# A written-out schedule with other costs, one more attention tile turned by VectorE, and another buffer for the first left operand

## The chip, the cores and the metric

The kernel runs on one core of a Trainium2 chip. The metric is device time in microseconds of one execution; of several executions the median is given. A profile is one more execution, taken by the hardware profiler; its span runs from the first to the last instruction. The five engines named below are TensorE (PE; its weight loads are shown as PEld), VectorE (DVE), ScalarE (ACT), GpSimd (POOL) and SyncE (SP), which issues all of this kernel's DMAs.

## The reference, cut to what matters

One layer of a hybrid encoder over a prompt of 1024 tokens and a sample of 32, width 1024. Normalised rows are multiplied by `w_in` into eight blocks of 512 columns (q, k, v and gate g of the head groups A and B, 8 heads of 64 each). Group A is chunked band attention with a relative bias, group B is stick-breaking attention. Both outputs are gated, multiplied by `w_out`, normalised and added; a last gated term with `w_ple_gate` and `w_ple` follows. Everything is float32.

```python
def stick_breaking(q, k, v, q_pos, k_pos):          # group B
    z = jnp.einsum('bqhd,bkhd->bhqk', q, k).astype(jnp.float32) * ATTN_SCALE
    causal = (k_pos[None, :] < q_pos[:, None])[None, None]
    log_1m = jnp.where(causal, jax.nn.log_sigmoid(-z), 0.0)
    after = lax.cumsum(log_1m, axis=3, reverse=True) - log_1m
    w = jnp.where(causal, jnp.exp(jax.nn.log_sigmoid(z) + after), 0.0).astype(v.dtype)
    return jnp.einsum('bhqk,bkhd->bqhd', w, v)
```

## The kernel before, in words

**Precision.** Every operand x of a matmul is split into hi (x rounded to the type fp32r) and lo (x - hi). ScalarE mostly casts hi, VectorE or GpSimd subtracts for lo, and TensorE adds up three products, or two where the halves are stacked.

**Stages.** First the rows are normalised and turned (`ptx`), and a part of the `w_ple` products is made (`ple`). Then come eight pairs of heads in the order A0, B0, A1, B1, A2, B2, A3, B3. While a pair's attention runs, the projections of the next pair (`mm_k..`, `mm_q..`, `mm_v..`, three column groups of 24 matmuls each) are woven in; beside the last pair stand the gates `mm_gA` and `mm_gB`. Last come the remaining `ple` products, the output projection (`o..P`) and the gate (`g..P`), each as seven products of half-size blocks (Strassen's way) for pairs of row tiles.

**Attention of one head** (`attention`, L790). A query tile i has 128 rows. `scores(i)` (L826) multiplies it with its keys into PSUM (tag S); for B, ScalarE takes a sigmoid into a tile `om`, VectorE scans it from right to left (cumulative product), and GpSimd subtracts neighbours into a tile `be`, the weights. `weights_t(i)` (L876) turns the weights, since the values product needs keys on partitions: TensorE transposes each 128x128 block into PSUM (tag T, named `ptw`), ScalarE casts hi (`wTh`), VectorE subtracts lo (`wTl`). For the tiles listed in `ROUND` (L31) another way is taken: VectorE transposes 32x32 squares from `be` back into `om`, one DMA writes `om` to DRAM (`swap`), four DMAs read it back into `be` with the squares in their turned places, and ScalarE and VectorE split it from there. `values(g)` (L926) multiplies four tiles at once with v (`PV`, `ot`). Tiles of `om` and `be` lie in two rings of fixed size (`Arena`, L208); a new tile waits for the last use of those that it overlaps. A B head's tile i has (i + 1) x 128 columns. The last head takes its tiles from 7 down to 0.

**The order of the work.** Nothing is issued as it is written. A `Recorder` (L264) collects all operations with their dependences; `cost` (L338) gives each a busy time and a time `late` from the end of that to the result; `order` (L372) then lists them: the engine that is free earliest takes the ready operation with the lowest key, where a result for another engine counts `SEM` = 60 ns more and for TensorE `MARGIN` = 400 ns more. On TensorE, attention goes before projections. The list is emitted as it stands, so each engine's instructions, and SP's DMAs, run in that fixed order. Line L450 in the profile is the one that emits everything; so instructions are known by their tiles' names.

**The output projection's start.** Raw weights `wo` are loaded into two buffers of tag `ao` in the pool `fb`, which opens when the attention's pool closes, and are split from there (L1451 on; `woB` and `woT` in turn, four each, two halves in each). The left operands of the even row tile (`A11o`, `A12o`, `S2o`, ...) are taken by `Side.room` (L1539) in turn from the same two buffers of `fb`, or from one buffer of `fa`, a pool that opens when the normalised rows are needed no more, behind the last gate projection.

Of the kernel before, what the change touches and what calls it, by code (L numbers as in the profile page):

```python
# [8 lines left out]
F32 = mybir.dt.float32  # L9
# [18 lines left out]

ROUND = {"A": ((4,),(6,)), "B": ((4,),(6,))}  # L31
LAG_T = 2
LAG_V = 2
SPACE_S = 0.1
# [229 lines left out]
class Recorder:  # L264
# [72 lines left out]
    @staticmethod  # L337
    def cost(eng, method, args, kw, writes, reads):  # L338

        out = writes[0] if writes else None  # L340
        n = out.free() if isinstance(out, View) else 1
        psum = any(isinstance(v, (View, Segments)) and v.buf.psum for v in reads)
        if eng == "PE":
            if method == "transpose":
                return (109 if args[1].shape[0] > 64 else 62), 165
            return max(109.0, 2.5 + 0.449 * args[2].free()) * (1 if args[2].buf.dtype == F32R else 4), 165
        if eng == "ACT":
            return (165 if psum else 200) + 0.83 * n + (190 if "accum_out" in kw else 0), 0
        if eng == "DVE":
            if method == "tensor_tensor_scan":  # L350
                return 155 + 2.08 * n, 0
            if method == "tensor_copy" and not psum:
                return 155 + 0.53 * n, 0
            if method == "scalar_tensor_tensor":
                return 210 + 1.04 * n, 0
            return 155 + 1.04 * n + (83 if method == "tensor_tensor_reduce" else 0), 0
        if eng == "POOL":
            if method == "tensor_tensor":
                if n == 1:
                    return 400, 0  # L360
                return 190 + (1.77 if out.buf.dtype == F32 else 2.15) * n, 0
            if method == "tensor_scalar":
                return 255 + 0.86 * n, 0
            return 100 + 0.82 * n, 0
        size, run = 4, 0
        for v in (out, args[1]):
            if isinstance(v, View) and v.buf.pool is not None:
                size, run = 4 * v.shape[0] * v.free(), 4 * v.shape[-1]
        return ISSUE, max(size / DMA_RATE, size / run * (8.5 + 0.0365 * run) / 16)


    def order(self):  # L372

        import heapq
        for place, old in self.turns:
            place.after.update(x[0] for x in old.uses)
        users = {id(o): [] for o in self.ops}
        for o in self.ops:
            o.left, o.ready = len(o.after), 0.0
            for a in o.after:  # L380
                users[id(a)].append(o)
        names = ("PE", "ACT", "DVE", "POOL", "SP", "CTL")
        free = dict.fromkeys(names, 0.0)
        soon = {e: [] for e in names}
        now = {e: [] for e in names}
        for o in self.ops:
            if not o.left:
                heapq.heappush(soon[o.eng], (0.0, o.key, id(o), o))
        out, port, line = [], 0.0, 0.0
        while len(out) < len(self.ops):  # L390
            best = None
            for e in names:
                if now[e]:
                    t = free[e]
                elif soon[e]:
                    t = max(free[e], soon[e][0][0])
                else:
                    continue
                if best is None or t < best[0]:
                    best = (t, e)  # L400
            t, e = best
            while soon[e] and soon[e][0][0] <= t:
                _, key, n, o = heapq.heappop(soon[e])
                heapq.heappush(now[e], (key, n, o))
            o = heapq.heappop(now[e])[2]
            if o.shared and e == "DVE" and port > t + DVE_SET:
                held = [x for x in now[e] if not x[2].shared]
                if held:
                    heapq.heappush(now[e], (o.key, id(o), o))
                    pick = min(held)  # L410
                    now[e].remove(pick)
                    heapq.heapify(now[e])
                    o = pick[2]
            o.at = t
            if e == "CTL":
                done = t
            elif e == "SP":
                free[e] = t + o.busy
                line = max(line, t + o.busy + DMA_NS) + o.late
                done = line + DMA_MARGIN  # L420
            else:
                if o.shared:
                    t = max(t, port - (DVE_SET if e == "DVE" else POOL_SET))
                    port = t + o.busy
                free[e] = t + o.busy
                done = t + o.busy + o.late
            out.append(o)
            for u in users[id(o)]:
                if u.eng == e and e != "SP":
                    r = t if e == "CTL" else free[e]  # L430
                else:
                    r = done + (0 if u.eng == "CTL" else SEM + (MARGIN if u.eng == "PE" else 0))
                u.ready = max(u.ready, r)
                u.left -= 1
                if not u.left:
                    heapq.heappush(soon[u.eng], (u.ready, u.key, id(u), u))
        return out
# [18 lines left out]
def stream_step(  # L456
# [19 lines left out]
    def scratch(shape, name):  # L476
# [29 lines left out]
        out=maskb, in_=maskb, pattern=[[-1, P]], base=0, channel_multiplier=1,  # L506
# [29 lines left out]
    def load_w(j):  # L536

        if j >= len(order) or j in raws:
            return
        kind, p = order[j]  # L540
        c0 = NAMES.index(kind) * 512 + p * P
        raws[j] = []
        for kh in range(2):
            raw = wpool.tile([P, 4, P], F32, tag="wr", name=f"wr_{kind}{p}_{kh}", bufs=4)
            dma(raw, w_in[0, kh * 512:(kh + 1) * 512, c0:c0 + P].rearrange("(k p) c -> p k c", p=P))
            raws[j].append(raw)

    def ensure(j):

        if j >= len(order) or j in loaded:  # L550
            return
        load_w(j)
        kind, p = order[j]
        loaded[j] = []
        if j == 2:
            pair = [ringl.tile([P, 2, 4, P], f"w{x}_{kind}{p}") for x in "hl"]
        for kh in range(2):
            raw = raws[j][kh]
            if j == 2:
                hi, lo = (x[:, kh] for x in pair)  # L560
            else:
                hi = wpool.tile([P, 4, P], F32R, tag="wh", name=f"wh_{kind}{p}_{kh}", bufs=4)
                lo = wpool.tile([P, 4, P], F32R, tag="wl", name=f"wl_{kind}{p}_{kh}", bufs=4)
            (nc.gpsimd.tensor_copy if j < 3 else nc.scalar.copy)(hi, raw)
            nc.gpsimd.tensor_tensor(lo, raw, f(hi), ALU.subtract)
            loaded[j].append((hi, lo))
# [223 lines left out]
    def attention(ab, p, h):  # L790
# [16 lines left out]

        together = {i: g for g in ROUND[ab] for i in g}
        whole, done_with = {}, []
# [4 lines left out]
        def rooms(i):  # L814

            more = ab == "B"
            g = together.get(i, (i,))
            if g not in whole:
                n = sum(cost(x) for x in g) * P
                whole[g] = ring0.tile([P, n + more * len(g)], f"om{nm}_{i}"), ring1.tile([P, n], f"be{nm}_{i}")  # L820
            k, n = g.index(i), cost(i) * P
            a = sum(cost(x) for x in g[:k]) * P
            w0, w1 = whole[g]
            return w0[:, a + more * k:a + more * k + n + more], w1[:, a:a + n]
# [379 lines left out]
    for n in range(-1, 8):  # L1204
        a = len(order)
        if n < 7:
            ab, p = pairs[n + 1]
            order += [(k + ab, p) for k in "kqv"]
        for _ in range(share.get(n, 0)):
            order.append(gates.pop(0))  # L1210
        span.append((a, len(order)))

    done = set()
# [309 lines left out]
    class Side:  # L1523
# [14 lines left out]

        def room(self, n, key):  # L1539
            if self.pair == 0:  # L1540
                one = Side.taken % 3 == 2
                Side.taken += 1
                x = (fa if one else fb).tile([P, 2, KT, P], F32R, tag="ao", name=f"{key}{self.nm}", bufs=1 if one else 2)
                return x[:, 0], x[:, 1]
            return [wpool.tile([P, KT, P], F32R, tag=tag, name=f"{tag}{key}{self.nm}", bufs=4) for tag in ("wh", "wl")]
# [321 lines left out]
```

## Time and profile before

| | |
|---|---|
| median of 3 executions | 806.38 us (805.48 to 808.88) |
| the profiled execution | 808.3 us, span 806.5 us |
| mean granted TensorE clock in it | 0.996 |
| busy: TensorE, VectorE, ScalarE, GpSimd | 784.5, 575.5, 507.8, 436.8 us |
| moved by DMA | 161.08 MB in 160971 packets, mean 200 GB/s |

The profiled execution takes 1.8 us more than its span. A busy time is the share of the span in which at least one instruction of that engine runs; matmuls overlap, so a group's busy time is less than its count times the mean duration. In the rows of groups, "xcount | busy, mean ns | idle before" follow the tiles and shapes; the idle time is that of the engine just ahead of these instructions, with what ended it. In rows of time, the start in us is followed by the length of the merged instructions. A row of waits has the total, the number of times and the longest.

### The profile page before, as it was taken

The page shows a single profiled execution, that of the slowest core. Times are in us where ns is not written, and L with a number is a line of the kernel's source. Part 1 is how long each engine was busy: PE and PEld are TensorE (multiplying, and loading weights), DVE is VectorE, ACT ScalarE, POOL GpSimd, SP SyncE. Part 2 cuts the span into 40 slices and gives each one's busy share as a digit, 9 for nine tenths or more (in the row PEclk, how much of TensorE's full clock was granted, in tenths as well). Part 3 has the DMA queues.
Part 4 walks back from the last instruction along what each step waited for, and adds up shares of the span by engine and source line. Part 5 has one row for each costly group of instructions (what it writes and reads, how often), then busy time and mean ns, then how long its engine had stood idle before and what let it go on. Part 6 is the DMA issues. An engine that isn't in the chain of part 4 may idle for free.

```text
span 806.5 us, 14268 instructions
## 1 busy us (share of the span) xinstructions
PE 784.5 (97%) x4646; PEld 722.4 (90%) x4646; DVE 575.5 (71%) x1007; ACT 507.8 (63%) x1063; POOL 436.8 (54%) x503
## 2 busy tenths in 40 slices
PE   8999999999999999999999999999998999999997
PEld 6899989999889998999999989999996877888786
DVE  6627678886588897778896878766355687586565
ACT  5636675676476655785666685543337867876741
POOL 5613656873556676234660336777541537699523
PEclk9999999999999999999999999999999999999999
DMA  8419987668877749745545667774579767659743
GB/s 275 152 38 276 232 247 243 168 181 237 229 210 228 203 147 272 190 137 152 125 115 159 153 171 231 218 211 151 156 236 329 245 188 231 216 179 343 249 137 131
DMA packets 160971, 161.08 MB, mean 200 GB/s; under 512 B 39153, under 2 KB 120793, under 8 KB 160898
## 3 DMA queue, kind: packets, MB, share of 16 engines
q1 hardware_dynamic: 160898, 160.18, 67.0%
q8 instruction: 37, 0.61, 0.3%
q14 instruction: 36, 0.29, 0.1%
HBM read 99.23 MB, written 52.49 MB: 188 GB/s over the span
## 4 chain that ended last, share of the span: by engine, by line
PE 84%; ACT 5%; POOL 3%; DVE 3%; DMA 2%; issue 2%; SPq 1%; DVEq 0%; ACTq 0%; POOLq 0%
PE mm_gB L450 6%; PE mm_gA L450 6%; PE mm_qA L450 5%; PE mm_kA L450 5%; PE mm_vA L450 5%; PE mm_qB L450 4%; PE mm_kB L450 4%; PE SB L450 4%; PE PVB L450 4%; PE mm_vB L450 3%; PE PVA L450 3%; PE SA L450 3%; PE ptwB L450 3%; PE o0P L450 3%; PE o1P L450 2%; PE g0P L450 2%
## 5 line engine op out<-in xcount | busy, mean ns | idle before, releaser
L450 DVE TENSOR_TENSOR_SCAN om<-om,SB 128x384 f32<-128x384 f32 (+5 forms) x96 | 95.6, 1005 | 12.1 <-ACT om L450 9.8
L450 POOL TENSOR_TENSOR be<-om 128x128 f32<-128x128 f32 (+7 forms) x64 | 77.5, 1216 | 49.4 <-DVE om L450 23.1
L450 ACT ACTIVATE om<-SB 128x384 f32<-128x384 f32 (+5 forms) x96 | 44.9, 494 | 29.9 <-DVE SB L450 17.7
L450 ACT ACTIVATE be<-om,statA 128x640 f32<-128x640 f32 (+3 forms) x64 | 44.5, 696 | 12.1 <-DVE statA L450 6.9
L450 ACT CAST wTh<-ptwB 128x512 fp32r<-128x512 f32 (+3 forms) x64 | 29.4, 482 | 21.1 <-PE ptwB L450 16.2
L450 DVE TENSOR_TENSOR wTl<-be,wTh 128x640 fp32r<-128x640 f32 (+1 forms) x32 | 35.5, 1108 | 7.1 <-ACT wTh L450 6.8
L450 DVE TENSOR_TENSOR wTl<-ptwB,wTh 128x512 fp32r<-128x512 f32 (+3 forms) x64 | 33.5, 545 | 7.7 <-ACT wTh L450 4.6
L450 DVE TENSOR_TENSOR wTl<-ptwA,wTh 128x512 fp32r<-128x512 f32 (+2 forms) x64 | 29.8, 482 | 11.6 <-ACT wTh L450 10.1
L450 PE MATMUL SB<-kdB,LB 128*128 128x384 f32 (+5 forms) x96 | 33.7, 354 | 1.9 <-DVE om L450 1.9
L450 DVE CUSTOM_DVE_ANT_0 om<-SA,biasA 128x320 f32<-128x320 f32 (+3 forms) x64 | 30.0, 483 | 6.2 <-PE SA L450 5.8
L450 PE MATMUL SB<-klB,LB 128*128 128x384 f32 (+5 forms) x96 | 32.9, 347 | 0.0
L450 DVE STREAM_TRANSPOSE om<-be 128x640 f32<-128x640 f32 (+1 forms) x32 | 28.8, 900 | 4.7 <-ACT be L450 2.3
L450 ACT CAST wTh<-ptwA 128x512 fp32r<-128x512 f32 (+2 forms) x64 | 26.1, 424 | 9.0 <-PE ptwA L450 8.2
L450 PE MATMUL SA<-kdA,LA 128*128 128x320 f32 (+2 forms) x96 | 30.0, 322 | 1.3 <-DVE LA L450 0.7
L450 POOL TENSOR_TENSOR sggA<-sggA,oggA 128x352 f32<-128x352 f32 x24 | 23.9, 997 | 13.6 <-DVE sggA L450 10.2
L450 POOL TENSOR_TENSOR oB<-oB,oB 128x256 f32<-128x256 f32 x32 | 24.4, 783 | 12.0 <-DMA oB<-in_w_out_dram 5.8
L450 PE MATMUL SA<-klA,LA 128*128 128x320 f32 (+2 forms) x96 | 29.3, 316 | 0.0
L450 PE MATMUL ptwB<-ident,be 128*128 128x128 f32 x192 | 29.3, 273 | 0.0
L450 ACT CAST wTh<-be 128x640 fp32r<-128x640 f32 (+1 forms) x32 | 24.9, 779 | 6.4 <-DMA be<-swapA 3.8
L450 PE MATMUL ptwA<-ident,be 128*128 128x128 f32 x160 | 26.8, 274 | 2.0 <-ACT be L450 1.3
L450 POOL TENSOR_TENSOR gB<-gB,gB 128x256 f32<-128x256 f32 x32 | 24.3, 783 | 4.7 <-DMA gB<-in_w_ple_gate_dram 4.3
L450 DVE TENSOR_TENSOR SB<-SB,maskb 128x128 f32<-128x128 f32 x64 | 17.6, 290 | 11.3 <-PE SB L450 11.1
(707 smaller groups left out, 2659.7 us busy)
## 6 DMA issues: line engine op xcount, KB each, us to landing
swapA<-om SPq DMA_DIRECT2D x16, 320.0 KB, 2.7
be<-swapA SPq DMA_DIRECT2D x64, 80.0 KB, 3.2
oB<-in_w_out_dram SPq DMA_DIRECT2D x16, 256.0 KB, 4.6
sum_dro<-oB SPq DMA_DIRECT2D x16, 256.0 KB, 3.8
gB<-in_w_ple_gate_dram SPq DMA_DIRECT2D x16, 256.0 KB, 4.2
sum_drg<-gB SPq DMA_DIRECT2D x16, 256.0 KB, 3.0
x<-in_x_prompt_dram SPq DMA_DIRECT2D x16, 256.0 KB, 4.0
h_dr<-h SPq DMA_DIRECT2D x8, 512.0 KB, 3.2
```

Source lines behind the costliest of these rows:

```text
L450: getattr(getattr(tc.nc, o.what[0]), o.what[1])(*args, **kw)
```

## The change

Four edits. Query tile 5 of each B head joins the tiles turned by squares and a transfer, as a group of its own beside 4 and 6. In `cost`, the fixed part of most ScalarE and VectorE operations is divided into a smaller busy part and a time `late`; GpSimd's tensor_tensor gets other constants. In `order`, a user on the same engine (other than TensorE) becomes ready with the result and not when the engine is free. In `Side.room`, the first, fourth, ... left operand of the even tile comes from `fa`, no longer the third, sixth, ...

```diff
-ROUND = {"A": ((4,),(6,)), "B": ((4,),(6,))}
+ROUND = {"A": ((4,),(6,)), "B": ((4,),(5,),(6,))}
...
         if eng == "ACT":
-            return (165 if psum else 200) + 0.83 * n + (190 if "accum_out" in kw else 0), 0
+            return (60 if psum else 95) + 0.83 * n + (190 if "accum_out" in kw else 0), 105
         if eng == "DVE":
             if method == "tensor_tensor_scan":
-                return 155 + 2.08 * n, 0
+                return 120 + 2.1 * n, 85
             if method == "tensor_copy" and not psum:
-                return 155 + 0.53 * n, 0
+                return 70 + 0.53 * n, 85
             if method == "scalar_tensor_tensor":
-                return 210 + 1.04 * n, 0
-            return 155 + 1.04 * n + (83 if method == "tensor_tensor_reduce" else 0), 0
+                return 125 + 1.04 * n, 85
+            if method == "tensor_tensor_reduce":
+                return 90 + 1.04 * n, 150
+            return 70 + 1.04 * n, 85
         if eng == "POOL":
             if method == "tensor_tensor":
                 if n == 1:
-                    return 400, 0
-                return 190 + (1.77 if out.buf.dtype == F32 else 2.15) * n, 0
+                    return 535, 40
+                return 170 + (1.77 if out.buf.dtype == F32 else 2.15) * n, 40
...
                 if u.eng == e and e != "SP":
-                    r = t if e == "CTL" else free[e]
+                    r = t if e == "CTL" else free[e] if e == "PE" else done
...
             if self.pair == 0:
-                one = Side.taken % 3 == 2
+                one = Side.taken % 3 == 0
```

In the built program, against before: TensorE has 48 transposes less; VectorE has 16 subtractions from PSUM less and 8 square transposes and 8 subtractions from SBUF more; ScalarE has 16 copies from PSUM less and 8 from SBUF more; SP issues 40 DMAs more; GpSimd's list is the same. The order differs on every engine. The rings' layout is the same.

## The prediction

> **What bounds the kernel now.** I read the page's first and second parts and its chain of waits first.
>
> ```profile
> span 806.5 us, 14268 instructions
> PE 784.5 (97%) x4646; PEld 722.4 (90%) x4646; DVE 575.5 (71%) x1007; ACT 507.8 (63%) x1063; POOL 436.8 (54%) x503
> PE 84%; ACT 5%; POOL 3%; DVE 3%; DMA 2%; issue 2%; SPq 1%; DVEq 0%; ACTq 0%; POOLq 0%
> ```
>
> TensorE works almost without a break, and the chain that ends last is mostly its matmuls. So only two things shorten this kernel: less TensorE work, or fewer breaks in it. Next comes the view of TensorE's waits, whose longest rows are these:
>
> ```profile
> PE o0P L450 <- ACT A11o L450: 2.5, 1, 2.5
> PE ptx L450 <- DVE be L450: 2.2, 2, 1.3
> PE SB L450 <- DVE om L450: 1.9, 3, 1.1
> PE mm_kB L450 <- ACT stvA L450: 1.5, 1, 1.5
> PE PVA L450 <- ACT wTh L450: 1.3, 1, 1.3
> ```
>
> One wait of 2.5 us stands where the output projection starts (o0P). The others are short and come from many places: the order written for each engine does not quite fit what the chip does. The view by windows tells where the breaks are:
>
> ```profile
> 363.00:446.00 83.00, 83.00 (x531) 80.44 (x531) 69.37 (x114) 54.57 (x115) 36.42 (x40) 1.00 0.48 137
> 484.00:590.00 106.00, 106.00 (x677) 103.65 (x676) 67.84 (x107) 46.00 (x102) 72.74 (x76) 1.00 0.64 193
> 40.00:600.00 560.00, 550.46 (x3529) 531.84 (x3528) 411.81 (x748) 344.38 (x736) 300.91 (x351) 1.00 0.67 190
> 600.00:807.00 207.00, 198.55 (x917) 159.62 (x915) 136.25 (x217) 138.50 (x280) 111.71 (x106) 0.98 0.69 224
> ```
>
> (Columns: stretch and length, then busy time of PE, PEld, DVE, ACT, POOL.) In the stretches of B's third and fourth pair TensorE has no gap at all, and from 40 to 600 us it stands idle for 560 - 550.46 = 9.5 us in all. The start and the tail are left by this change as they are.
>
> **The change, part by part.** *Tile 5 of B.* In each of 8 heads, six transposes on TensorE go (48 in the built program's order, nothing else on TensorE). What is one worth? The grouped view and the timeline give different answers:
>
> ```profile
> L450 PE MATMUL ptwB<-ident,be 128*128 128x128 f32 x192 | 29.3, 273 | 0.0
> 131.68 0.82 PE L450 MATMUL ptwB<-ident,be 128*128 128x128 f32 x6
> 132.25 1.54 PE L450 MATMUL mm_kA<-hnh,wh_kA 128*128 128x352 f32 x8
> 133.63 0.32 PE L450 MATMUL mm_kA<-hnh,wl_kA 128*128 128x352 f32 x1
> 592.40 1.46 PE L450 MATMUL mm_gB<-hnl,wh_gB 128*128 128x352 f32 x8
> 593.70 0.49 PE L450 MATMUL mm_gB<-hnh,wh_gB 128*128 128x352 f32 x2
> ```
>
> A transpose lasts 273 ns, but they overlap: from the first of six (131.68) to the next matmul (132.25) there are 0.57 us, 95 ns each. The eight matmuls behind them take 133.63 - 132.25 = 1.38 us, where eight undisturbed ones take 593.70 - 592.40 = 1.30: another 0.08. So a tile is worth 0.65 us, and eight are worth 8 x 0.65 = 5.2 us. The bounds: 48 x 0.095 = 4.6 if nothing is lost behind a group, 48 x 29.3/192 = 7.3 by the group's busy time. I take 5.2, since what ends later is the next matmul's start.
>
> The Trainium skill, "TensorE: Matmul & The Clock Gate", Part 4 on the transpose, gives about 275 ns for one in a kernel; the trace's 273 agrees as a duration. Counted as occupancy it would give 48 x 0.275 = 13.2 us, and the timeline speaks against that.
>
> What replaces them:
>
> ```profile
> L450 DVE STREAM_TRANSPOSE om<-be 128x640 f32<-128x640 f32 x24 | 20.0, 833 | 2.9 <-ACT be L450 2.3 <-POOL be L450 0.4
> L450 DVE STREAM_TRANSPOSE om<-be 128x896 f32<-128x896 f32 x8 | 8.8, 1102 | 1.8 <-POOL be L450 1.6
> L450 DVE TENSOR_TENSOR wTl<-be,wTh 128x640 fp32r<-128x640 f32 x24 | 25.1, 1044 | 3.6 <-ACT wTh L450 3.3
> L450 DVE TENSOR_TENSOR wTl<-be,wTh 128x896 fp32r<-128x896 f32 x8 | 10.4, 1301 | 3.5 <-ACT wTh L450 3.5
> L450 DVE TENSOR_TENSOR wTl<-ptwB,wTh 128x512 fp32r<-128x512 f32 x32 | 21.4, 681 | 6.3 <-ACT wTh L450 3.3 <-PE PVB L450 2.8
> L450 DVE TENSOR_TENSOR wTl<-ptwB,wTh 128x256 fp32r<-128x256 f32 x16 | 6.5, 409 | 0.3 <-ACT wTh L450 0.3
> ```
>
> Tile 5 has 768 columns, midway between 640 and 896: squares (833 + 1102)/2 = 0.97 us, subtraction (1044 + 1301)/2 = 1.17, against 0.68 + 0.41 = 1.09 that go. VectorE gets 1.05 us more per head, 8.4 in all. From 363 to 446 us it is busy for 69.37 of 83 us; two heads make that 71.5 of some 81.7, 87%. TensorE, with its projections queued between the attention's steps, still covers this; uncovered, up to 8.4 us would come back. ScalarE's two copies become one of the same columns, and save a fixed part at most: nothing. The transfers are 8 x (384 KB out, 384 KB back) = 6.3 MB beside 161, and 40 more issues on SP's queue. They stand behind other SP work in the built order, and the values product that needs tile 5 also needs tile 7, which is scored two tiles later. I put them at nothing; the slower rival prices the opposite.
>
> *The scheduler's costs.* No instruction changes; the order on all engines does. Are the new prices nearer to the chip?
>
> ```profile
> 609.91 1.29 DVE L450 TENSOR_TENSOR oB<-woB,oB 128x512 fp32r<-128x512 f32 x2 [2.58 <-ACT oB L450]
> 609.26 1.14 ACT L450 CAST oB<-woB 128x512 fp32r<-128x512 f32 x2
> L450 DVE TENSOR_TENSOR oB<-woB,oB 128x512 fp32r<-128x512 f32 x8 | 5.3, 687 | 4.3 <-ACT oB L450 4.3
> L450 ACT CAST oB<-woB 128x512 fp32r<-128x512 f32 x8 | 4.7, 619 | 1.6 <-DMA woB<-in_w_out_dram 1.6
> ```
>
> Two subtractions of 687 ns end after 1.29 us, so the second starts 0.60 after the first; the new formula says 70 + 1.04 x 512 = 602 and 85 on top, the old one 687 of occupancy. Two casts of 619 need 1.14: 0.52 apart; new 95 + 0.83 x 512 = 520 and 105, old 625. So the old model made both engines too slow, by about 0.1 us an instruction, and thereby put TensorE's steps late, with slack; the new one is right on both and leaves less slack. In the new order the longest run of attention matmuls without a projection matmul between, at the start of the second A pair's sample step, is dissolved; steps of the third A pair move back by up to 60 projection matmuls. I see no net sign: bounds are all of the 9.5 us between 40 and 600 gone, and as much again added. I take zero.
>
> *The other room.* The left operand A11 of the first product had a buffer of the kind that the raw weights wo use; now it takes the one that is free as soon as the projections end.
>
> ```profile
> 619.01 0.39 PE L450 MATMUL ple<-wpl1False,php 128*64 128x512 f32 x1
> 621.89 0.99 PE L450 MATMUL o0P<-oB,A11o 128*128 128x512 f32 x2 [2.50 <-ACT A11o L450]
> 621.22 0.62 ACT L450 CAST A11o<-uo 128x512 fp32r<-128x512 f32 x1 [0.32 <-DVE oB L450]
> 619.91 1.28 DVE L450 TENSOR_TENSOR oB<-woB,oB 128x512 fp32r<-128x512 f32 x2
> 611.58 0.93 SPq L450 DMA_DIRECT2D woB<-in_w_out_dram  x2
> woB<-in_w_out_dram SPq DMA_DIRECT2D x8, 256.0 KB, 3.5
> ```
>
> A11's cast waited for the last raw weights' subtraction (619.91, 1.28 long) and started at 621.22; TensorE waited 2.5 us. That wait goes. Late next are the last quarter's weights, on which three of the product's twelve matmuls hang. In the new order the attention's last values product stands 39 projection matmuls later (39 x 0.162 = 6.3 us), so the pool with the raw weights opens that much later: the last load, issued 7.7 us ahead of 619.3 now (611.58), would be issued 1.4 ahead, land at +2.1, and be cast and subtracted by about +4. TensorE has 18 matmuls that do without it (18 x 0.23 = 4.1 us). So it just fits; I take 1.5 of the 2.5 us (ends: 0 and 2.5).
>
> Sum: 5.2 + 0 + 1.5 = 6.7 us off the profiled execution's own 808.3 us (span 806.5). That run stands 1.9 above the median of 806.4 of the runs shown, so the forecast against the median is 806.4 - 6.7 = 799.7.
>
> **The rivals.**
> 1. *The new order keeps the gain small.* With less slack, waits such as mm_kB on stvA or PVA on wTh (1.3 to 1.5 us each) become more. The 9.5 us of idle time growing by half, 4.7, leaves 6.7 - 4.7 = 2.0: 804.4. For it: the model's prices are now without reserve. Against: it is nearer to the chip.
> 2. *The new order also closes the gaps.* Half of the 9.5 and all of the 2.5 go: 5.2 + 4.7 + 2.5 = 12.4, 794.0.
> 3. *Slower: a slot that is held too long.* In the rings om and be, tiles 1 to 3 of the next head lie over tile 5 of this one. Until now om's place was free once POOL had subtracted and be's once TensorE had transposed; now be's is held for squares, out, back, cast and subtraction. With these rows
>
> ```profile
> swapB<-om SPq DMA_DIRECT2D x8, 320.0 KB, 3.8
> be<-swapB SPq DMA_DIRECT2D x32, 112.0 KB, 3.5
> L450 ACT CAST wTh<-be 128x896 fp32r<-128x896 f32 x8 | 7.5, 942 | 1.8 <-DMA be<-swapB 1.8
> L450 DVE TENSOR_TENSOR_SCAN om<-om,SB 128x512 f32<-128x512 f32 x24 | 30.5, 1270 | 1.9 <-ACT om L450 0.9 <-POOL om L450 0.8
> ```
>
> that is 0.97 + 3.8 + 3.5 + 0.9 + 1.2 = 10.4 us. In the new order VectorE has two scans of 1.27, the squares of tile 6 and some small steps between, about 6 us, before the next head's tiles 1 and 2. Where TensorE has no projection matmuls for the missing 4 us, it stands: at half of that in 8 heads 16 us, less 6.7, so +9: 816. It decides from the point where the hold outlasts the projections queued between; the gapless stretches speak against it.
> 4. *A transpose is worth its 273 ns.* 48 x 0.273 = 13.1, with the room 14.6: 791.8. The timeline's 95 ns speak against it. That no transposes go is ruled out by the built order.
>
> **How the numbers follow.** About 0.5%, 4 us, is what a measurement of this kernel can tell from no change: faster means under 802.4, slower over 810.4. Forecast 0.45 (797 to 802.4), rival 2 0.12, rival 4 0.03: faster 0.60. Rival 1 0.24: same. Rival 3 0.16: slower. The range leaves out rivals 3 and 4 with 0.19: from 793.5, rival 2's time, to 809, where the idle time of 9.5 us has doubled (806.4 - 6.7 + 9.5 = 809.2).
>
> **What would show it.** TensorE 48 matmuls fewer, its chain share unchanged; the wait of o0P for A11o gone or moved to oB; swapB 40 issues more; VectorE about 8 us busier; idle time of TensorE from 40 to 600 us near 9.5. Wrong is the forecast if that idle time grows by over 5 us, or if waits of om or be for swapB appear ahead of the next head's tiles.

## The result, and the profile after

| | before | after |
|---|---|---|
| median, same chip | 805.99 us (6 runs) | 812.34 us (810.45 to 813.27, 6 runs) |
| ratio, 95% interval | | 1.0071 [1.0056, 1.0086] |
| profiled execution, span | 808.3, 806.5 us | 813.3, 811.5 us |
| granted TensorE clock | 0.996 | 0.997 |
| moved by DMA | 161.08 MB | 167.38 MB |

The changed kernel is 0.7% slower, where 0.8% faster was forecast; its 812.3 us lie above the range's upper end of 809. The page of after, its span, busy times and chain:

```profile
span 811.5 us, 14255 instructions
PE 786.0 (97%) x4598; PEld 717.6 (88%) x4598; DVE 589.6 (73%) x1007; ACT 504.5 (62%) x1055; POOL 437.7 (54%) x503
PE 72%; DMA 8%; ACT 7%; POOL 4%; DVE 4%; issue 3%; SPq 2%; ACTq 0%; DVEq 0%; POOLq 0%
```

48 matmuls are gone, yet TensorE's busy time has grown from 784.5 to 786.0 us, and its share of the chain fell from 84% to 72%: DMA and ScalarE have taken the place. TensorE's waits in after:

```profile
PE SB L452 <- DVE om L452: 3.3, 4, 1.5
PE ptwA L452 <- ACT be L452: 2.2, 3, 1.3
PE ptwA L452 <- DVE wTl L452: 2.0, 1, 2.0
PE o0P L452 <- ACT A12o L452: 1.3, 1, 1.3
PE pth L452 <- DMA ht<-h_dr: 1.3, 1, 1.3
PE mm_vB L452 <- ACT wh_vB L452: 1.3, 1, 1.3
PE mm_kB L452 <- ACT wh_kB L452: 1.2, 1, 1.2
```

The 2.5 us of o0P for A11o are gone, as the room was meant to do (o0P now waits 1.3 us for A12o, its next operand). But several rows of 1 to 3 us in total are new or longer, most of them while the attention runs. The windows of after (stretch, length, then busy PE, PEld, DVE, ACT, POOL, the granted clock, DMA share, GB/s):

```profile
40.00:600.00 560.00, 545.03 (x3439) 520.64 (x3438) 418.29 (x740) 338.63 (x721) 300.07 (x348) 1.00 0.70 196
600.00:812.00 212.00, 203.69 (x951) 163.73 (x950) 142.98 (x223) 140.88 (x286) 113.03 (x108) 0.99 0.70 231
```

Between 40 and 600 us TensorE is idle for 560 - 545.03 = 15.0 us, where it was 9.5: 5.4 us more, over the 5 us that the prediction named as its refutation.

Idle time shows only half of it. A matmul's shown length runs past the start of the next, so a short wait is counted as busy. I therefore took every matmul's start from the trace of before, and for each width of operand the median distance to the next start. The sum of these medians over a kernel's matmuls is the time of TensorE's work without any wait; what the starts are apart beyond that is lost (that also holds long ends such as the ones behind narrow transposes, the same in all kernels).

| start to start, us | work | lost | of it from 40 to 600 us | start of the last matmul against before |
|---|---|---|---|---|
| before | 772.7 | 26.8 | 15.6 | |
| after | 767.5 | 37.4 | 27.7 | +5.5 |

TensorE's work fell by 5.2 us, as the forecast has it for the transposes (with after's own medians it is 767.6). Lost time grew by 10.6, and between 40 and 600 us by 12.0. So the question is what made 10 us of lost time.

A second thing hides in TensorE's busy time. For some stretches the trace grants TensorE half its clock, each time behind a break. Before has one behind the wait of o0P, after has one at another place (windows as above):

```profile
622.20:625.60 3.40, 3.40 (x9) 2.65 (x8) 3.40 (x4) 2.33 (x6) 2.63 (x2) 0.50 1.14 344
116.40:119.80 3.40, 3.40 (x15) 3.40 (x13) 2.96 (x5) 2.49 (x6) 3.40 (x5) 0.50 0.56 166
```

The first row is of before, the second of after. A matmul takes about twice as long there, as rows further down show, so such a stretch costs up to half its length. Before and after have 3.4 us of it each: it moves, but doesn't make the difference between these two.

### The profile page after: what moved, and what is told of

It is laid out like the page before. It is cut to its first block, busy times and chain, and to the rows that moved or that the text cites. A ratio compares the mean times of both kernels' runs of the same rounds, so it can differ in the third digit from the quotient of the medians.

```text
span 811.5 us, 14255 instructions
## 1 busy us (share of the span) xinstructions
PE 786.0 (97%) x4598; PEld 717.6 (88%) x4598; DVE 589.6 (73%) x1007; ACT 504.5 (62%) x1055; POOL 437.7 (54%) x503
## 2 busy tenths in 40 slices
DMA packets 166733, 167.38 MB, mean 206 GB/s; under 512 B 39793, under 2 KB 125529, under 8 KB 166658
## 4 chain that ended last, share of the span: by engine, by line
PE 72%; DMA 8%; ACT 7%; POOL 4%; DVE 4%; issue 3%; SPq 2%; ACTq 0%; DVEq 0%; POOLq 0%
PE mm_gB L452 6%; PE mm_gA L452 6%; PE mm_kA L452 5%; PE mm_vA L452 5%; PE mm_qA L452 5%; PE PVB L452 4%; PE SB L452 3%; PE mm_qB L452 3%; PE mm_vB L452 3%; PE mm_kB L452 3%; PE PVA L452 2%; PE g0P L452 2%; PE g1P L452 2%; PE g2P L452 2%; PE g3P L452 2%
## 5 line engine op out<-in xcount | busy, mean ns | idle before, releaser
L452 POOL TENSOR_TENSOR be<-om 128x896 f32<-128x896 f32 (+7 forms) x64 | 75.7, 1189 | 69.3 <-DVE om L452 25.9
L452 DVE TENSOR_TENSOR wTl<-be,wTh 128x640 fp32r<-128x640 f32 (+2 forms) x40 | 48.9, 1227 | 9.9 <-ACT wTh L452 8.2
L452 ACT ACTIVATE be<-om,statA 128x640 f32<-128x640 f32 (+4 forms) x64 | 44.3, 694 | 11.6 <-DVE statA L452 6.7
L452 DVE STREAM_TRANSPOSE om<-be 128x640 f32<-128x640 f32 (+2 forms) x40 | 36.6, 914 | 7.1 <-POOL be L452 3.4
L452 DVE CUSTOM_DVE_ANT_0 om<-SA,biasA 128x320 f32<-128x320 f32 (+3 forms) x64 | 29.7, 482 | 10.6 <-PE SA L452 7.1
L452 ACT CAST wTh<-be 128x640 fp32r<-128x640 f32 (+2 forms) x40 | 31.4, 791 | 9.0 <-DMA be<-swapA 4.6
L452 POOL TENSOR_TENSOR oB<-oB,oB 128x256 f32<-128x256 f32 x32 | 25.7, 824 | 20.7 <-issue 9.0
L452 ACT CAST wTh<-ptwB 128x512 fp32r<-128x512 f32 (+3 forms) x48 | 21.9, 481 | 19.5 <-PE ptwB L452 16.1
L452 POOL TENSOR_TENSOR gB<-gB,gB 128x256 f32<-128x256 f32 x32 | 26.7, 851 | 8.5 <-DMA gB<-in_w_ple_gate_dram 6.0
L452 POOL TENSOR_TENSOR sggA<-sggA,oggA 128x352 f32<-128x352 f32 x24 | 24.4, 1018 | 10.6 <-DVE sggA L452 6.5
L452 DVE TENSOR_TENSOR wTl<-ptwB,wTh 128x512 fp32r<-128x512 f32 (+3 forms) x48 | 25.4, 545 | 4.5 <-ACT wTh L452 4.2
L452 POOL TENSOR_TENSOR klB<-stkB,kdB 64x1024 fp32r<-64x1024 f32 x8 | 19.2, 2405 | 16.9 <-ACT kdB L452 8.8
L452 PEld LDWEIGHTS ptwA<-ident,be 128*128 128x128 f32 x160 | 19.1, 141 | 7.8 <-ACT be L452 3.0
```

What stands on the lines that cost most here:

```text
L452: getattr(getattr(tc.nc, o.what[0]), o.what[1])(*args, **kw)
```

## The experiments

Each kernel was compared with the kernel before on the same chip. Here are all of them; "kept order" means that the list of before was emitted as it stood, with only the named instructions taken out or put in. "Lost" is as above; work is 772.7 us with the 48 transposes and 767.5 without. "Half clock" is for how many us, between 20 us and the last matmul, the clock stood at 0.50. Both are of one profiled execution, which can lie 2 to 3 us off the median (e17's 2.7 below, e18's 2.1 above, before's 2.3 above).

| run | median us | ratio to before [95%] | lost | half clock |
|---|---|---|---|---|
| e1 tile 5 alone, replanned | 828.2 | 1.0254 [1.0221, 1.0286] | 53.2 | 23.9 |
| e2 costs alone | 808.9 | 1.0036 [1.0019, 1.0053] | 27.2 | 0 |
| e3 room alone | 803.0 | 0.9954 [0.9934, 0.9974] | 21.1 | 0 |
| e7 costs and room | 805.3 | 0.9990 [0.9977, 1.0003] | 24.5 | 0 |
| e4 before, MARGIN 440 | 820.9 | 1.0160 [1.0126, 1.0194] | 39.3 | 17.1 |
| e15 before, MARGIN 360 | 805.7 | 0.9991 [0.9980, 1.0003] | 25.7 | 3.4 |
| e12 after, MARGIN 440 | 825.6 | 1.0250 [1.0214, 1.0286] | 48.6 | 13.7 |
| e16 after, MARGIN 360 | 817.6 | 1.0139 [1.0122, 1.0156] | 40.5 | 6.8 |
| e6 kept order, tile 5 not turned | 805.5 | 0.9991 [0.9972, 1.0010] | 29.3 | 3.4 |
| e14 e6 and 40 tiny transfers | 812.1 | 1.0080 [1.0051, 1.0109] | 36.6 | 6.8 |
| e13 e6 and 40 full transfers, no wait | 817.9 | 1.0138 [1.0121, 1.0155] | 42.5 | 6.8 |
| e10 e6 and the 40 transfers, nobody reads | 836.9 | 1.0372 [1.0344, 1.0400] | 60.8 | 30.7 |
| e9 kept order, squares, no transfers | 814.2 | 1.0100 [1.0068, 1.0132] | 35.9 | 0 |
| e5 kept order, the whole detour | 840.4 | 1.0422 [1.0400, 1.0444] | 64.1 | 27.3 |
| e11 e5, return transfers later | 831.0 | 1.0298 [1.0271, 1.0324] | 55.8 | 20.5 |
| e8 room and e5 | 836.2 | 1.0361 [1.0337, 1.0386] | 61.9 | 23.9 |
| e17 after without the 40 transfers | 814.0 | 1.0085 [1.0055, 1.0115] | 35.1 | 3.4 |
| e18 e17 without the squares | 812.1 | 1.0062 [1.0040, 1.0084] | 38.0 | 6.8 |

**The parts one by one.** e1 takes the first edit alone, e2 the costs and the rule for the same engine, e3 the room, e7 both of these.

```diff
-ROUND = {"A": ((4,),(6,)), "B": ((4,),(6,))}
+ROUND = {"A": ((4,),(6,)), "B": ((4,),(5,),(6,))}
```

> Before with the tile-5 edit alone. Costs theory (the new prices leave TensorE's steps without slack and cost 10 us): this kernel keeps the old prices, so it gains the transposes' 5 us: 801, ratio 0.994. Tile theory (the detour through squares and a transfer costs more than the transposes): slower, about 811 to 816, ratio 1.006 to 1.012. Draw theory (every new order loses by chance against the order of before): 803 to 808.

> Before with the new costs and the same-engine rule alone. Costs theory: the 10 us of lost TensorE time appear here, 814 to 817, ratio 1.010 to 1.014. Tile theory: 805 to 807, ratio 1.00. Draw theory: 808 to 813.

```diff
-                one = Side.taken % 3 == 2
+                one = Side.taken % 3 == 0
```

> Before with the other buffer for the left operands alone. The prediction's term says 804.5 (1.5 us of the 2.5 us wait of o0P for A11o go), ratio 0.998, and that wait is gone from TensorE's list. If the last weights are late instead, the wait stays at 2 to 2.5 us under another name: 806, ratio 1.00. Draw theory: the order up to the output projection should hardly change here, so the same as the costs theory.

> After without the tile-5 edit. If the edits add up (costs alone +2.4 us, room alone -3.5): 804 to 806, ratio 0.998 to 1.000, and tile 5 then costs 7 us beside them. Order theory: may fall anywhere from 803 to 815, since the order is made anew. Tile theory: 804 to 806.

The room gives 0.46%, 3.7 us, the costs take 0.36%, 2.9 us, and the two together make 0.999: they add. Tile 5 takes 2.5%, 20 us, when planned with the old costs, and 0.71 + 0.10 = 0.81%, 6.5 us, beside the other edits (812.3 against 805.3). The kernel with the room alone is the fastest of all. In e2 TensorE still waits at the output projection, and in e3 that row is gone:

```profile
PE o0P L452 <- ACT A11o L452: 2.3, 1, 2.3
```

**Is it the order that is drawn?** e4 changes one constant of the planner by a tenth and so nothing but the order; e12, e15 and e16 were added later.

```diff
-MARGIN = 400
+MARGIN = 440
```

> Before with MARGIN, the slack that the scheduler adds ahead of TensorE's steps, at 440 instead of 400 ns and nothing else: a small push that gives another order of the same work. Costs theory and tile theory: within 1.5 us of before, 804.5 to 807.5. Draw theory (before has a lucky order): 808 to 814 with lost TensorE time up by 3 to 8 us.

> The kernel before with MARGIN 360: another order, nothing else. e4 (440) was 15 us above the kernel before. If before's order is a lucky one among its neighbours: 810 to 825. If 400 is a plain optimum of a smooth curve: 806 to 812.

> The changed kernel with MARGIN 440 in place of 400, which alters nothing but the order. If the result of the changed kernel is mostly a matter of which order the planner happens to draw, this lies anywhere from 803 to 822, and may come out below before. If the detour of tile 5 costs a firm 7 us in any order planned with the new costs, 810 to 822.

> The changed kernel with MARGIN 360: another order, nothing else. If the changed kernel's time is one draw of a wide spread: anywhere from 803 to 830, and against e15 no firm sign. If tile 5's detour costs a firm amount in every order: above e15 by 5 us or more, as at 400 (6 us) and 440 (5 us).

The order alone moves the kernel before from 805.7 to 820.9 us, and the changed one from 812.3 to 825.6. In e4 the instructions are before's, and lost time grows by 12.5 us. It lies in new waits and in what follows them: the clock stands at 0.50 for 17.1 us, where before has 3.4, which can be (17.1 - 3.4) / 2, some 7 of the 12.5. The longest waits of e4:

```profile
PE ptwA L450 <- ACT be L450: 4.0, 1, 4.0
PE mm_kB L450 <- ACT stvA L450: 3.3, 1, 3.3
PE g0P L450 <- DVE uu L450: 2.5, 1, 2.5
```

At the same margin the changed kernel is slower in all three pairs: by 817.6 - 805.7 = 11.9, 6.3 and 825.6 - 820.9 = 4.7 us. The clock doesn't make that: lost time grows by 14.8, 10.6 and 9.3 us, and the stretches at 0.50 by 3.4, 0 and -3.4. Before's order at 400 is not a lonely lucky draw, since 360 is as good.

**The detour in the kept order.** To see tile 5 without a new order, e5 emits before's list, leaves out the recorded operations of tile 5's turning, puts the squares and the transfers where `be` is ready by the plan, and the cast and the subtraction 9 us later. e6 leaves the detour out and splits the unturned weights: that part of the output is not the reference's. e8 is e5 with the room.

```diff
+            real.vector.transpose(sq.rearrange("p (c b q) -> p b c q", c=4, q=32), bk)
+            real.sync.dma_start(d, sq)
+            for c in range(4):
+                x = d[:, c * m * 32:(c + 1) * m * 32].rearrange("(g k) x -> k g x", k=32)
+                real.sync.dma_start(bk[32 * c:32 * c + 32].rearrange("k (g x) -> k g x", g=4), x)
...
+            tc.nc.scalar.copy(h, src)
+            tc.nc.vector.tensor_tensor(l, src, h.bitcast(F32), ALU.subtract)
```

> Before, scheduled as before with tile 5's transposes in the plan; only when the list is written out, those transposes, their casts and subtractions are left out, and squares, transfer, cast and subtraction of tile 5 are put in: the squares when the weights are planned ready, cast and subtraction 9 us of planned time later. Everything else keeps its place. Order theory (the detour costs nothing, the new order that the scheduler makes of it does): 800 to 802.5, ratio 0.993 to 0.996. Tile theory (VectorE's extra microsecond a head, 40 transfers on SP's queue or the held ring slots cost more than the transposes): 808 to 820.

> Before in its own order with the turning of tile 5 of B left out: no transposes and no transfer; hi and lo are taken from the weights as they lie, so this part of the output is not the reference's. It prices the 48 transposes alone. Both theories: 800 to 802, ratio 0.993 to 0.995 (5.2 us of the prediction). If freed TensorE time is given back at the next wait: 804 to 806.

> The room edit with its own order, and tile 5 put in afterwards as in the run with the kept order. Order theory: the gains add up, 803.0 - 5 = 798, ratio 0.989 to 0.992. Tile theory: 805 to 816.

e6 is the first surprise: 48 transposes less and nothing in their place, and the kernel is 0.7 us faster, within its interval of no change. The work fell by 5.2 us, lost time rose by 2.5 (26.8 to 29.3), and the two profiled spans differ by 806.5 - 803.8 = 2.7. In a fixed list TensorE comes earlier to the next wait, and much of what it saved is lost again. e5 is the second: 34 us slower. Two waits on SyncE's queue are new in it (line, tile, then total, times, longest):

```profile
SPq L1004 <- DMA swapB<-om: 19.7, 8, 4.7
SPq L1001 <- DVE om L1000: 10.4, 7, 3.4
```

L1004 issues the four return transfers. They must wait until the outward one (L1001) has landed, which itself waits for the squares, and everything that SyncE has to issue behind them waits too.

**The detour taken apart.** e9 makes the squares and the late split, without any transfer. e10 makes the transfers without squares, on to a place in DRAM that nobody reads; e13 lets the returns read an input, so that nothing waits; e14 moves almost no bytes. Where squares or transfers are missing, tile 5 is split unturned, and that part of the output is not the reference's. e11 is e5 with the returns some 4 us later by the plan.

```diff
-            real.vector.transpose(sq.rearrange("p (c b q) -> p b c q", c=4, q=32), bk)
-            real.sync.dma_start(d, sq)
+            real.sync.dma_start(d, bk)
...
-                real.sync.dma_start(bk[32 * c:32 * c + 32].rearrange("k (g x) -> k g x", g=4), x)
+                real.sync.dma_start(e[32 * c:32 * c + 32].rearrange("k (g x) -> k g x", g=4), x)
```

> The order of before kept; tile 5 of B gets its squares on VectorE and is cast and subtracted from SBUF 9 us later by the plan, but none of the 40 transfers is made, so what is split is not the turned tile and the output part is not the reference's. Theory Q (SyncE's queue, in order, stands while a return transfer waits for its outward one, and everything behind it comes late): without transfers nearly all of the 34 us goes, 803 to 810. Theory V (VectorE's extra microsecond a head, in an order that has no place for it, and the later split): most of the loss stays, 825 to 840. A mixture lies between, and its size gives VectorE's part.

> The order of before kept; tile 5 of B isn't turned and is split from the weights as they lie (as in e6, so the output part is not the reference's), and beside it the 40 transfers are issued on SyncE's queue at the place that they have in e5, from the weights to DRAM and on to a second place in DRAM, where nobody reads them. No engine waits for their data and VectorE has no squares. Theory Q: SyncE's queue still stands during each outward transfer, so most of the loss is here, 825 to 840. Theory V: 805 to 810, as in e6 (805.5).

> As e5 (the order of before kept, tile 5 of B turned by squares and transfers, whole computation), but the four return transfers are issued about 4 us later by the plan than the outward one, and the split 7 us after that. SyncE then finds the outward transfer landed. Theory Q: SyncE's wait for swapB at these lines falls from 19.7 to below 5 us and the time by 15 us or more, 806 to 825. Theory V: time stays at 832 to 842, whatever SyncE waits for.

> As e10 (order of before, tile 5 of B not turned, 40 transfers that nobody reads; output part not the reference's), but the four return transfers read an input of the kernel instead of what the outward one wrote: same bytes, same pieces, same 40 issues, and no wait of SyncE for the outward transfer. If the wait of SyncE's queue makes e10's loss (836.9 against e6's 805.5): 806 to 815. If the traffic or the issues make it: 825 to 838.

> As e13, but each of the 40 transfers moves 32 (outward) or 8 numbers (returns) a piece, so 40 issues and almost no bytes, and no wait of SyncE. If the issues themselves cost, it stands near e13; if bytes cost, it is near e6 (805 to 808) while e13 is well above it. If the wait alone costs, both are near e6.

The steps from e6, in shares of before: 40 issues +0.9% (e14), their bytes +0.6% (e13), the wait for the outward transfer +2.3% (e10): 7, 5 and 19 us. The squares with the late split make +1.1%, 9 us (e9). The parts don't add up to e5 (7 + 5 + 19 + 9 = 40 against 34.8 from e6 to e5): some of it hides some other. Nor are the 19 us all flight: e10 has the clock at 0.50 for 30.7 us and e13 for 6.8, which can be (30.7 - 6.8) / 2 = 12 of them. e11 lies between its two theories: SyncE waits no more for swapB at the return's line, and 9.5 us come back, not 15. Where the rest stays isn't shown; tile 5's cast and subtraction wait 3.9 and 4.0 us once each for the later data.

One place of e10 shows how a transfer that nobody reads stops TensorE. SyncE's queue, where L1009 is the outward, L1012 the return, L489 all the rest:

```profile
303.35 0.93 SPq L489 DMA_DIRECT2D wr_kB<-in_w_in_dram  x2
304.38 0.45 SPq L1009 DMA_DIRECT2D swapB<-be  x1
308.04 2.50 SPq L1012 DMA_DIRECT2D deadB<-swapB  x4
310.64 0.52 SPq L489 DMA_DIRECT2D swapB<-om  x1
```

The same place in before:

```profile
297.22 0.93 SPq L450 DMA_DIRECT2D wr_kB<-in_w_in_dram  x2
298.25 0.45 SPq L450 DMA_DIRECT2D swapB<-om  x1
```

In before the next outward transfer, of a tile 4, is issued 1.0 us after the raw weights, in e10 7.3 us after: 0.5 for an issue, 3.2 of waiting, 2.5 for four issues. ScalarE in e10:

```profile
314.24 1.08 ACT L489 ACTIVATE om<-SB 128x512 f32<-128x512 f32 x2 [3.35 <-DMA swapB<-om]
317.03 0.43 ACT L489 COPY stvA<-mm_vA 128x352 f32<-128x352 f32 x1
```

The next sigmoid needs the place in the ring `om` that this late transfer still reads (3.35 us), and behind it in ScalarE's list, after a table load and an exponential, stands the copy of mm_vA out of PSUM. TensorE in e10, and its windows around the place:

```profile
310.99 1.46 PE L489 MATMUL mm_kB<-hnh,wh_kB 128*128 128x352 f32 x8
317.52 1.54 PE L489 MATMUL mm_kB<-hnh,wh_kB 128*128 128x352 f32 x4 [5.08 <-ACT stvA L489]
318.86 1.38 PE L489 MATMUL mm_kB<-hnh,wl_kB 128*128 128x352 f32 x4
322.38 1.65 PE L489 MATMUL mm_kB<-hnl,wh_kB 128*128 128x352 f32 x8
323.87 0.80 PE L489 MATMUL mm_kB<-hnh,wl_kB 128*128 128x352 f32 x4
```

```profile
317.50:321.00 3.50, 3.48 (x12) 3.48 (x13) 3.46 (x3) 1.01 (x2) 2.94 (x3) 0.50 0.67 176
321.00:325.00 4.00, 4.00 (x22) 4.00 (x21) 1.11 (x3) 1.18 (x2) 2.06 (x2) 0.77 0.98 286
```

TensorE stands for 5.08 us, and then pays once more: the granted clock is 0.50 for the next 3.5 us, where four matmuls take 318.86 - 317.52 = 1.34 us, twice what they take later (0.64 from 323.87, since the next matmul starts at 324.51).

The Trainium skill, "TensorE: Matmul & The Clock Gate", Part 1, says that the array falls to half rate after an idle window of about 3.4 us and comes back after being busy as long; this place agrees, with 5.08 us and 0.50. Shorter breaks did it as well: 2.50 us at o0P in before and 1.98 us in after, the two rows at 0.50 shown with the result; the 2.3 us at o0P in e2 did not. So in this kernel a break needn't last 3.4 us, and its length alone doesn't decide.

**The detour in the changed kernel's own order.** The prices above hold where the list has no place for the detour. The changed kernel's list was planned with it. e17 emits that list without the 40 transfers, e18 also without the squares; both split tile 5 unturned, so that part of the output is not the reference's.

```diff
+                if id(o) in self.alone:
+                    assert o.eng == "SP"
+                    continue
```

> The changed kernel in its own order, without the 40 transfers of tile 5 (the split reads the weights unturned, so the output part is not the reference's). If the 7 us that tile 5 costs beside the other edits (812.3 against e7's 805.3) are the transfers': 800 to 806. If they are VectorE's or the order's: 809 to 813.

> As e17, and VectorE's eight square transposes of tile 5 go too (8 x 0.97 us of VectorE). If VectorE's squares cost: 3 us or more below e17. If they are hidden: within 1 us of e17. If both stay at 809 or more, the order drawn is to blame; the tile that is not turned at all in the kept order gave 805.5, and with the room's 3.5 us 802.

814.0 and 812.1 against 812.3: the intervals overlap with after's, so in its own order neither the transfers nor the squares cost anything that can be measured. (Work taken out of a fixed list need not give its time back, as e6 shows. So these two runs say that this list sets the time, and e7 that a list planned without tile 5 is faster.) The waits of e18 are after's:

```profile
PE ptwA L456 <- ACT be L456: 2.2, 3, 1.3
PE SB L456 <- DVE om L456: 2.2, 4, 1.0
PE ptwA L456 <- DVE wTl L456: 2.1, 2, 1.9
PE mm_kB L456 <- ACT wh_kB L456: 1.6, 1, 1.6
```

And so are the places where it loses. Start of the first matmul of some tiles, and of the last matmul of all, less that in before:

| us in before | tile | after | e18 | e7 (no tile 5) |
|---|---|---|---|---|
| 122.6 | mm_kA of A1 | +4.6 | +4.6 | +3.5 |
| 165.0 | mm_vA of A1 | -3.5 | -3.5 | 0.0 |
| 244.7 | mm_kA of A2 | +3.5 | +2.9 | -1.5 |
| 419.0 | mm_kB of B3 | +7.4 | +6.0 | +1.4 |
| 483.9 | mm_gA | +7.0 | +5.9 | -0.5 |
| 621.9 | o0P | +3.0 | +1.9 | -3.1 |
| 800.8 | last matmul | +5.5 | +6.0 | -2.3 |

(A single start also moves because the order does; the last row is time.) So what the changed kernel loses is set by the list that the planner drew, with or without the work that the change adds. The longest wait of after in the attention shows the kind. TensorE in after, then VectorE, then ScalarE:

```profile
112.52 1.45 PE L452 MATMUL mm_vB<-hnh,wl_vB 128*128 128x352 f32 x8
115.95 0.95 PE L452 MATMUL ptwA<-ident,be 128*128 128x128 f32 x5 [1.98 <-DVE wTl L452]
116.56 2.69 PE L452 MATMUL mm_vB<-hnl,wh_vB 128*128 128x352 f32 x8
119.05 1.01 PE L452 MATMUL mm_vB<-hnh,wh_vB 128*128 128x352 f32 x3
```

```profile
114.35 0.82 DVE L452 TENSOR_TENSOR wTl<-be,wTh 128x640 fp32r<-128x640 f32 x1 [1.75 <-ACT wTh L452]
115.20 0.69 DVE L452 TENSOR_TENSOR wTl<-ptwA,wTh 128x512 fp32r<-128x512 f32 x1
```

```profile
110.54 0.58 ACT L452 COPY otA<-PVA 64x512 f32<-64x512 f32 x1
113.59 0.73 ACT L452 CAST wTh<-be 128x640 fp32r<-128x640 f32 x1 [2.47 <-DMA be<-swapA]
114.22 0.58 ACT L452 CAST wTh<-ptwA 128x512 fp32r<-128x512 f32 x1
```

ScalarE stands 2.47 us for a transfer of group A, which the change doesn't touch, and the cast that TensorE's next PSUM tile needs is behind it in the list; VectorE's subtraction follows, and TensorE waits 1.98 us. Projection matmuls that need none of this stand in its list only behind these transposes. Then the clock is at 0.50 until 119.8 us: eight of them take 119.05 - 116.56 = 2.49 us, where the prediction read 1.30 for eight. No instruction of tile 5 is in this chain, and e18, without the detour, waits 1.9 us at the same place: only the places in the list have changed. In before the same two casts stand the other way round, and neither waits:

```profile
113.76 0.58 ACT L450 CAST wTh<-ptwA 128x512 fp32r<-128x512 f32 x1
115.18 0.73 ACT L450 CAST wTh<-be 128x640 fp32r<-128x640 f32 x1
```

## Why the prediction was wrong

**Transposes, -5.2 us.** Right as work: 5.2 us by before's medians, and with each kernel's own ones 767.5 to 767.7 us without them against 772.7 to 773.8 with them. Wrong as time: the sum took each microsecond of TensorE's work off the end, and e6, where nothing else happens, got 0.7 us (interval -2.3 to +0.8) of 5.2. A chain that is 84% TensorE still holds waits whose date is set by another engine; a TensorE that is ready sooner waits longer there.

**Squares and subtractions, hidden.** Right. The durations were, too (0.97 and 1.17 us forecast):

```profile
L452 DVE STREAM_TRANSPOSE om<-be 128x768 f32<-128x768 f32 x8 | 7.7, 962 | 0.0
L452 DVE TENSOR_TENSOR wTl<-be,wTh 128x768 fp32r<-128x768 f32 x8 | 9.7, 1212 | 0.2 <-ACT wTh L452 0.2
```

e18 without the squares is not measurably faster than after. In an order that has no place for them they cost 9 us together with the later split (e9).

**Transfers and SyncE, at nothing.** Nothing measurable in the changed kernel's own order (e17). The reason given, that they stand behind other SyncE work, fits: SyncE's waits for an outward transfer of B are short there, where e5 has 19.7 us.

```profile
SPq L452 <- DMA swapB<-om: 2.5, 4, 1.3
```

Outside that order this was the dearest part by far: 31 us (e10).

**The scheduler's costs and the order, zero within 9.5 us.** This is the step that failed: "I see no net sign ... I take zero". The costs by themselves make +2.9 us (e2, inside the bounds), and with the room they end at before's time (e7). The list as it is drawn with tile 5's detour had no price of its own, and it is what costs: between 40 and 600 us lost time grows by 12.0 us, over the upper bound of 9.5. The new prices didn't make the list better either, though the rows of the prediction have them nearer to the chip: e2 is slower than before. And the bound was read from idle time alone (9.5 us), while the lost time of the same stretch was 15.6: short waits hide in TensorE's busy time.

**The room, -1.5.** Right in sign, too small alone: 3.7 us (interval 2.1 to 5.3), and the upper end was put at 2.5. The sum took the wait of o0P and not what follows it: from o0P's start on before loses another 1.5 us in the stretch at half clock, and e3, where the wait is gone, has no such stretch and loses nothing there. The clock of 0.98 from 600 to 807 us, in a row that the prediction shows, is in part this stretch. Beside the other edits nothing is left of the gain: after loses 4.0 us from o0P's start on, with 1.3 us for A12o and 1.3 for `pth`, where before loses 2.5 ahead of it and 1.5 behind.

**The rivals.** The first named the mechanism, a new order that keeps the gain small by more waits, at half the idle time, 4.7 us; it was 10.6 of lost time, and so the time ended on the other side. The third, a ring slot held by the transfer, is not borne out: ScalarE waits once, 2.0 us, for a place in `om` that a swapB transfer reads, and no longer in e17, whose transfers of tile 5 are gone; but TensorE's wait for om is 3.3 us in after and still 3.0 in e17, and e17 isn't faster. The fourth, 13 us for the transposes, is ruled out by 5.2 of work.

The sum as measured: work -5.2, lost +10.6, together 5.5 (by unrounded numbers) between the last matmuls of the two profiled executions, whose spans differ by 811.5 - 806.5 = 5.0. Of these +10.6, the costs and the room together account for 24.5 - 26.8 = -2.3 (e7), and planning with tile 5 for 37.4 - 24.5 = +12.9.

**What stays open.** Why the planner finds worse lists once tile 5 takes the detour. It did so in four of four (three margins, and the old costs in e1). Which of its inputs misleads it was not tried: it may be the price of a transfer, or the casts that stand in ScalarE's list ahead of other work while they wait for a transfer.

## What to carry to other kernels

In a kernel whose instructions run in written lists, a change has two prices: that of its instructions and that of the new list; freeze the old list, or take the added work out of the new one, to see them apart. Work taken off the busiest engine is worth only what the next date set by another engine lets through: count its gain in starts, not in busy time. A break on the busiest engine can cost more than its length, so look at the granted clock behind it. A transfer that depends on another one on the same queue costs everything behind it the first one's flight, unless other issues are put between.

## What the runs showed of the hardware

Issuing is not free on SyncE's queue. In e10 the view of the return's line gives (ns, min, median, max):

```profile
L1012 SPq DMA_DIRECT2D deadB<-swapB x32: 562/592/1477, 133.5 to 593.8; - x32
```

Four of them take 2.5 us, and 40 issues that move almost nothing cost the kernel 7 us (e14 against e6), more than the bytes of the full transfers do (e13 against e14: 5 us). A break on TensorE can cost more than its length: in e10 the granted clock is halved for 3.5 us behind a break of 5.08 us, in before for 3.4 us behind one of 2.50, in after behind one of 1.98, and not in e2 behind one of 2.3. The stretch in before costs 1.5 us; in e10 the mean clock over the run fell to 0.981. And busy time can grow while work shrinks: TensorE is busy 786.0 us with 48 matmuls less, against 784.5.
